# Modulation sums on TensorE, an earlier gather of expert rows, and another order of loads at the beginning

## The chip, the cores and the metric

The kernel runs on one core of a Trainium2 chip. The metric is the time of one execution on the device in microseconds (us). Five engines work side by side, each in the order of its own queue: PE (TensorE, matmuls into the eight banks of PSUM), DVE (VectorE), ACT (ScalarE), POOL (GpSimd) and SP (SyncE, which here only issues DMAs). Sixteen DMA engines move data between device memory and on-chip memory. A profile shows one execution; the share of full speed that the chip grants to PE is listed as PEclk (1.00 is 2.4 GHz, 0.50 is 1.2 GHz).

## What is computed

A trunk of two layers works on `x` (512 tokens of 1024 numbers, float32), steered by one vector `c` of 1024. Each layer derives six modulation vectors from `c`, mixes the tokens, and then sends each token through two of 32 experts:

```python
c_act = jax.nn.silu(c)
for layer in range(DEPTH):                       # two layers
    mod = c_act @ ada_w[layer] + ada_b[layer]    # 1024 x 6144 weights, 24 MB a layer
    shift1, scale1, gate1, shift2, scale2, gate2 = jnp.split(mod, 6, axis=-1)
    h = modulate(rmsnorm(x, norm1_w[layer]), shift1, scale1)
    # layer 0: h @ mix_w_in -> pooling channels, q, k, v; pooling and chunked attention; @ mix_w_out
    # layer 1: h @ ssm_w_in -> convolution, chunked state-space scan, gated norm; @ ssm_w_out
    x = x + gate1[:, None, :] * mix
    h2 = modulate(rmsnorm(x, norm2_w[layer]), shift2, scale2)
    # experts: top group of 4, top 2 of its 8 experts, silu(t @ w1) * (t @ w3), @ w2
    x = x + gate2[:, None, :] * ffn
return rmsnorm(x, final_norm_w)
```

## The kernel before

Tokens lie in four tiles of 128 rows. Most products of float32 numbers are split into a high and a low part of each operand (`split`, L108 to L113: ACT copies the high part, DVE or POOL subtracts to get the low one), and three matmuls add high by high, high by low and low by high. The framework orders the instructions of each engine by a model of costs, with the order of the program as priority; `manual_schedule` fixes the order by hand for the routing and for the end of each expert layer.

**Modulation.** A part of `ada_w` is 2048 columns wide. `ada` (L165) is a generator that loads eight pieces of 128 x 2048 (1 MB each) into a ring of five tiles (`w8`) and advances one piece at each call. A DVE instruction multiplies piece k by the column k of `c_act` and adds piece k-1; after the eighth, four matmuls with ones in 32 columns (L198) sum over the 128 partitions, and the bias row is added. In the even layer three such parts (`adas`: gate and router vectors of layer 0, and shift and scale of layer 1) are advanced at 25 places of the attention code (`fill`, with the counts in `FILL`). Two further parts run inside layer 1 and are not touched.

**The beginning (`even_mixer`).** SP issues the loads of `c`, of the four x tiles, of small vectors (`vrow`, `crow4`), and of the first 2048 modulation columns in two chunks of 512 + 512 columns (`ada_loads`), each followed by two loads of v weights. x is normalised and transposed by PE into `xa`; `ada_sums(b)` forms the sums of chunk b with the same DVE chain, `modulate(b)` applies them and splits the result into `h_hi` and `h_lo`; `v_products(b)` multiplies by the v weights: 8 pieces x 4 tiles x 3 matmuls. Then follow the dense products q0, k0, u0, u1, q1, ... (`Dense.next`, 24 matmuls each, L426 to L429), scores, transposes and values per pair of heads, and `out_proj` (`mo`). `late_loads` (L272 to L276) fetches three vectors of 32 numbers: `ssm_D` into `dcol`, number by number in a repeating pattern over 64 partitions twice, and `dtb` and `arow` repeated over 128 partitions. They are used in layer 1.

**Experts (`Moe.run`).** 17 units of two experts (16 pairs, and an overflow unit at position 8) run one after another. Unit u's hidden products come first, then `results(u - 1)`: y is written to the buffer `yd` in device memory, except for the units of the list `LAST` (units 8, 10, 13, 14, 15, 16), whose y is split and kept on chip with a one-hot matrix in `parts_y`. `products` multiplies the one-hot matrix by the kept y for each token tile, and `padd` (L1086) adds the result to x. For units 8, 10 and 13 this happens inside the loop two units later; units 14, 15 and 16 are the three operands of `combine` at the end. `ygather` (L1178) fetches the rows of `yd` by eight indirect DMAs on POOL that add into the four x tiles, two for each tile. It is issued in unit `GAT`. `combine` follows by hand: all products, then steps "x" (`padd`) and "h" (the next norm and transposes) in the order of `STEPS`. In layer 0, `ahead` loads and splits `wdt` (1024 rows of 32 numbers for layer 1) just before `combine`.

Of the kernel before, what the change touches and what calls it, by code (L numbers as in the profile page):

```python
# [36 lines left out]
GAT = 15  # L37
# [16 lines left out]
HOLD = 7  # L54
PINS = 3
# [7 lines left out]
LO = {"v": "G", "e": "VVG", "m": "V", "o": "GVV", "s": "VV"}  # L63
# [4 lines left out]
STEPS = "x0 h0 x1 h1 h0 x2 h2 h0 h1 x3 h2 h3 h3 h0 h1 h2 h1 w1 h3 w2 h3 h2"  # L68
# [7 lines left out]
def trunk_kernel(ctx, tc, x, c, ada_w, ada_b, norm1_w, norm2_w, mix_w_in, pool_w, pool_scale,  # L76
# [86 lines left out]

    def ada(layer, part, eng, first=None):
# [19 lines left out]
        load(1)  # L184
        for k in range(KD):
# [8 lines left out]
        for _ in range(SLACK):  # L194
            yield
        p = ps(name=f"pada{layer}{part}")
        for q in range(4):
            PE.matmul(p[32 * q:32 * q + 32, :], ones[:, 0:32], ws[KD - 1][:, q * 512:(q + 1) * 512], start=True,  # L198
                      stop=True, skip_group_check=True)
# [57 lines left out]
    pv = ps(name="pv")  # L257
    PE.transpose(pv[:, 0:P], vrow, ident)
    PE.transpose(pv[:, P:2 * P], crow4, ident)
    V.tensor_copy(vcol, pv[:, 0:P])  # L260
    V.tensor_scalar(cw.rearrange("p t k -> p (t k)"), pv[:, P:2 * P], 0.5, None, op0=ALU.mult)
# [4 lines left out]
    V.tensor_scalar(cb, vcol[:, 20:52], 0.5, None, op0=ALU.mult)  # L266
# [3 lines left out]

    def late_loads():
# [218 lines left out]
    def even_mixer(layer):  # L490
        with ExitStack() as es:
# [15 lines left out]
            def ada_loads(b):  # L507
                SP.dma_start(adb[0:64:32, b * 512:(b + 1) * 512], dap(ada_b, b * 512, [[D, 2], [1, 512]]))
                for k in range(0, KD, 2):
# [3 lines left out]
                    aw[b, k], aw[b, k + 1] = (t[:, d].rearrange("p q n -> p (q n)") for d in range(2))  # L513
# [26 lines left out]

            def modulate(b):
# [12 lines left out]
            def v_products(b):  # L554
                for kk in (4 * b, 4 * b + 2):
# [8 lines left out]
            def ada_sums(b):  # L564
                V.tensor_scalar(aw[b, 0], aw[b, 0], ccol[:, 0:1], None, op0=ALU.mult)
                for k in range(1, KD):
                    V.scalar_tensor_tensor(aw[b, k], aw[b, k], ccol[:, k:k + 1], aw[b, k - 1], op0=ALU.mult,
                                           op1=ALU.add)
                p = ps(name=f"pada00{b}")
                for q in range(2):  # L570
                    PE.matmul(p[32 * q:32 * q + 32, :], ones[:, 0:32], aw[b, KD - 1][:, q * 512:(q + 1) * 512],
                              start=True, stop=True, skip_group_check=True)
                m = adb[0:64, b * 512:(b + 1) * 512]
                V.tensor_add(m, p[0:64], m)
                p = ps((P, 4, 64), name=f"pm00{b}")
                for q in range(4):
                    PE.transpose(p[:, q, :], m[:, q * P:(q + 1) * P], ident[0:64, 0:64])
                ks = slice(4 * b, 4 * b + 4)
                V.scalar_tensor_tensor(ab[:, 0, 0, ks], p[:, :, 32], 1.0, n1w[0][:, ks], op0=ALU.add, op1=ALU.mult)
# [1225 lines left out]
```

## Time and profile before

| | |
|---|---|
| time, median of 3 runs | 1119.99 us (1119.96 to 1123.87) |
| profiled execution, its own time | 1120.03 us |
| its span, first to last instruction | 1118.3 us |
| mean granted PE clock | 0.932 |
| PE, DVE, ACT, POOL busy | 973.2, 800.3, 388.9, 300.2 us |
| DMA | 263.88 MB, mean 236 GB/s |

A line of the timeline gives start, duration, engine, line and operation, output <- inputs, shapes and, in brackets, how long the engine stood idle before and what released it. "x16" says that equal instructions in a row were merged. A float32 matmul that isn't split appears as two passes. A line with "q" after the engine's name (SPq) is an instruction that issues a DMA or waits.

### The profile page before, as it was taken

The page shows a single profiled execution, that of the slowest core. Times are in us where ns is not written, and L with a number is a line of the kernel's source. Part 1 is how long each engine was busy: PE and PEld are TensorE (multiplying, and loading weights), DVE is VectorE, ACT ScalarE, POOL GpSimd, SP SyncE. Part 2 cuts the span into 40 slices and gives each one's busy share as a digit, 9 for nine tenths or more (in the row PEclk, how much of TensorE's full clock was granted, in tenths as well). Part 3 has the DMA queues.
Part 4 walks back from the last instruction along what each step waited for, and adds up shares of the span by engine and source line. Part 5 has one row for each costly group of instructions (what it writes and reads, how often), then busy time and mean ns, then how long its engine had stood idle before and what let it go on. Part 6 is the DMA issues. An engine that isn't in the chain of part 4 may idle for free. (4 is left out here: it accounts for less than half of the span.)

```text
span 1118.3 us, 15578 instructions
## 1 busy us (share of the span) xinstructions
PE 973.2 (87%) x5474; PEld 729.5 (65%) x5474; DVE 800.3 (72%) x1650; ACT 388.9 (35%) x753; POOL 300.2 (27%) x329
## 2 busy tenths in 40 slices
PE   4588788699699996898999899899989999799994
PEld 3466466388556654776786777777766878556653
DVE  6717986654565874789997989887797555564976
ACT  3135332425123232433444333443433325222332
POOL 4413100204231122411513416244142004231124
PEclk9789888799799998899999999999999999799997
DMA  9476876598699979536473465554334945699987
GB/s 332 139 265 168 286 282 252 215 364 330 209 364 414 411 229 255 210 107 198 143 264 88 135 194 159 190 158 113 126 109 152 333 154 209 204 390 415 412 278 185
DMA packets 140200, 263.88 MB, mean 236 GB/s; under 512 B 19917, under 2 KB 82337, under 8 KB 134994
## 3 DMA queue, kind: packets, MB, share of 16 engines
q1 hardware_dynamic: 129122, 235.40, 60.1%
q0 software_dynamic: 8928, 20.97, 7.2%
q10 hardware_dynamic: 2064, 6.42, 1.4%
q8 instruction: 47, 0.77, 0.3%
q14 instruction: 39, 0.32, 0.1%
HBM read 254.19 MB, written 20.11 MB: 245 GB/s over the span
## 5 line engine op out<-in xcount | busy, mean ns | idle before, releaser
L1036 PE MATMUL ph<-w,xT 128*64 128x256 f32 (+1 forms) x1152 | 132.1, 374 | 0.9 <-DVE xT L1020 0.7
L1036 PEld LDWEIGHTS ph<-w,xT 128*64 128x64 f32 x1152 | 86.8, 139 | 51.8 <-issue 10.9
L189 DVE SCALAR_TENSOR_TENSOR ada<-ada,ccol,ada 128x2048 f32<-128x2048 f32 x35 | 87.1, 2489 | 0.2
L1003 POOL DMA_INDIRECT xg<-xnd,toks x32 | 32.3, 1008 | 149.8 <-PE pxt L1015 122.6
L1057 PE MATMUL pyy<-w,hidT 128*64 128x512 f32 x272 | 65.9, 605 | 4.2 <-ACT hidT L1049 4.2
L1038 ACT ACTIVATE th<-ph 128x128 f32<-128x128 f32 x34 | 9.4, 278 | 160.8 <-PE pht L1047 137.1
L1022 ACT ACTIVATE xT<-pxt,mc 128x128 f32<-128x128 f32 x136 | 51.3, 458 | 17.9 <-PE pxt L1015 10.9
L1062 DVE SCALAR_TENSOR_TENSOR y<-pyy,wsl,gate 128x512 f32<-128x512 f32 x68 | 48.1, 744 | 6.1 <-DMA yd<-y 4.5
L1015 PE MATMUL pxt<-ident,xg 128*128 128x128 f32 x272 | 37.9, 284 | 15.5 <-DVEq L1383 7.9
L1086 DVE TENSOR_TENSOR x<-x,pyc 128x512 f32<-128x512 f32 x64 | 40.4, 682 | 14.1 <-PE pyc L1079 8.0
L1039 DVE SCALAR_TENSOR_TENSOR th<-th,ph 128x128 f32<-128x128 f32 x34 | 9.8, 287 | 55.7 <-ACT th L1038 55.7
L1020 DVE TENSOR_SCALAR xT<-pxt,mc 128x128 f32<-128x128 f32 x136 | 46.6, 405 | 1.4 <-PE pxt L1015 1.4
L1581 DVE TENSOR_SCALAR ms<-lb,acs 128x128 f32<-128x128 f32 x128 | 41.0, 359 | 5.9 <-DMA lb<-acd 3.6
L1015 PEld LDWEIGHTS pxt<-ident,xg 128*128 128x128 f32 x272 | 34.5, 194 | 16.2 <-issue 15.6
L1548 DVE SCALAR_TENSOR_TENSOR cvx<-pdx,cw,cvx 128x511 f32<-128x511 f32 (+2 forms) x48 | 35.4, 738 | 6.7 <-ACT cvx L1545 6.6
L1178 POOL DMA_INDIRECT x<-yd,row x16 | 25.1, 1571 | 50.0 <-DMA xgfw<-in_final_norm_w_dram 22.3
L1584 POOL TENSOR_TENSOR ms<-ms,cbm 128x512 f32<-128x512 f32 x16 | 32.0, 2001 | 17.8 <-ACT ms L1583 16.0
L1057 PEld LDWEIGHTS pyy<-w,hidT 128*64 128x64 f32 x272 | 16.5, 136 | 28.1 <-issue 19.4
L1079 PE MATMUL pyc<-yh,yot 128*128 128x512 f32 x128 | 33.7, 398 | 1.0 <-DVE yot L1070 1.0
L469 DVE TENSOR_TENSOR sor<-sor,gate 128x1024 f32<-128x1024 f32 x16 | 20.4, 1276 | 18.0 <-DMA sor<-in_ssm_w_out_dram 17.9
L661 ACT ACTIVATE scs<-scs,mx 128x512 f32<-128x512 f32 (+3 forms) x32 | 17.7, 555 | 36.2 <-DVE mx L660 32.8
L1079 PEld LDWEIGHTS pyc<-yh,yot 128*128 128x128 f32 x128 | 23.4, 188 | 9.6 <-issue 1.9
(1074 smaller groups left out, 2778.4 us busy)
## 6 DMA issues: line engine op xcount, KB each, us to landing
w<-in_moe_w_dram SPq DMA_DIRECT2D x192, 512.0 KB
ada<-in_ada_w_dram SPq DMA_DIRECT2D x40, 1024.0 KB
yd<-y SPq DMA_DIRECT2D x22, 512.0 KB
ada<-in_ada_w_dram SPq DMA_DIRECT2D x16, 512.0 KB
wx<-in_ssm_w_in_dram SPq DMA_DIRECT2D x16, 512.0 KB
wz<-in_ssm_w_in_dram SPq DMA_DIRECT2D x16, 512.0 KB
lb<-acd SPq DMA_DIRECT2D x32, 256.0 KB
sor<-in_ssm_w_out_dram SPq DMA_DIRECT2D x16, 512.0 KB
```

What stands on the lines that cost most here:

```text
L189: a = eng.scalar_tensor_tensor(ws[k], ws[k], ccol[:, k:k + 1], ws[k - 1], op0=ALU.mult, op1=ALU.add)
L1003: d = GP.indirect_dma_start(out=xg, out_offset=None, in_=xnd[:, :], in_offset=bass.IndirectOffsetOnAxis(ap=idx, axis=0), bounds_check=T - ...
L1015: PE.transpose(p[:, q, :], xv[:, 4 * hf + q, :], ident)
L1020: V.tensor_scalar(xT[:, k, :], p[:, q, :], a, b, op0=ALU.mult, op1=ALU.add)
L1022: S.activation(xT[:, k, :], p[:, q, :], AF.Identity, bias=b, scale=a)
L1036: PE.matmul(ph[64 * j:64 * j + 64, n:n + h, :], xT[:, k, 64 * j:64 * j + 64], w13[n][:, :, k, :], start=k == 0, stop=k == KD - 1, skip_gro ...
L1057: PE.matmul(py[64 * j:64 * j + 64], hT[:, 64 * j:64 * j + 64], w2[:, s], start=True, stop=True, skip_group_check=True)
L1062: V.scalar_tensor_tensor(y[:, s], py, self.wsl[:, slot:slot + 1], self.gate2[:, s], op0=ALU.mult, op1=ALU.mult)
L1079: PE.matmul(p, part[2][:, i * P:(i + 1) * P], part[hf][:, q * 512:(q + 1) * 512], start=n + q == 0, stop=n == len(parts) - 1 and q == 1)
L1086: V.tensor_add(xst["x"][i][:, s], xst["x"][i][:, s], p)
L1548: V.scalar_tensor_tensor(a[:, sh:], p[:, :T - sh], cw[:, tap, ch:ch + 1], a[:, sh:], op0=ALU.mult, op1=ALU.add)
L1581: V.tensor_scalar(ms[:, h, :], lb[:, h, :], acs[:, cq, 4 * g + h:4 * g + h + 1], 0.0, op0=ALU.subtract, op1=ALU.min)
```

## The change

In the beginning and in the three parts of the even layer the modulation sums are formed by PE alone: the stationary operand is the column of `c_act` repeated 32 times, the moving operand the weights as loaded, and PSUM accumulates over the eight pieces. The two parts of layer 1 stay as they were. In the beginning the two pieces of a pair go to different groups of PSUM partitions, and the two halves are added after the transposes. The three short vectors are loaded as rows of 128 bytes into one partition and spread over the partitions by a product with ones. The transposes of the small vectors (`columns`) and the bias rows come later in the program; `ada_sums(1)` comes ahead of the v products; the low parts of the v weights and of all of h are subtracted by DVE. In the expert layers the gather is issued in unit 14, unit 13 becomes a fourth operand of `combine`, with the last operand separate for tiles 0 and 1, and two tiles come from the ring `w8`. In layer 0, `wdt` is loaded in unit 10 into another buffer and split by POOL at a new step `w0`.

```diff
-GAT = 15
+GAT = 14
+EARLY = 10
-LO = {"v": "G", "e": "VVG", "m": "V", "o": "GVV", "s": "VV"}
+LO = {"v": "V", "e": "VVG", "m": "V", "o": "GVV", "s": "VV"}
-STEPS = "x0 h0 x1 h1 h0 x2 h2 h0 h1 x3 h2 h3 h3 h0 h1 h2 h1 w1 h3 w2 h3 h2"
+STEPS = "x0 h0 x1 h1 h0 x2 h2 h0 h1 x3 h2 h3 h3 h0 h1 h2 h1 w0 w1 h3 w2 h3 h2"
...
+    def ada_mm(p, k, w, first, last):
+
+        for q in range(4):
+            PE.matmul(p[32 * q:32 * q + 32, :], ccol[:, k:k + 1].to_broadcast([P, 32]), w[:, q * 512:(q + 1) * 512],
+                      start=first, stop=last, skip_group_check=True)
...
             load(k + 2)
             yield
+            if not eng:
+                if not k:
+                    p = ps(name=f"pada{layer}{part}")
+                ada_mm(p, k, ws.pop(k), k == 0, k == KD - 1)
+                continue
...
+    def columns():
+
+        pv = ps(name="pv")
+        PE.transpose(pv[:, 0:P], vrow, ident)
+        PE.transpose(pv[:, P:2 * P], crow4, ident)
...
     def late_loads():
         SP.dma_start(yd[len(MAIN) * P:, :], zrow)
+        hrow = st_.tile([1, 3, 32], F32, name="hrow")
+        for n, src in enumerate((ssm_D, ssm_dt_bias, ssm_A_log)):
+            SP.dma_start(hrow[:, n, :], dap(src, 0, [[0, 1], [1, 32]]))
+        return hrow
+
+    def head_rows(hrow):
+
+        p = ps((P, 3, 32), name="phr")
+        PE.matmul(p, ones[0:1, :], hrow, start=True, stop=True)
         for q in range(2):
-            SP.dma_start(dcol[64 * q:64 * q + 64, :], dap(ssm_D, q, [[0, 64], [2, 16]]))
-        SP.dma_start(dtb, dap(ssm_dt_bias, 0, [[0, P], [1, 32]]))
-        SP.dma_start(arow, dap(ssm_A_log, 0, [[0, P], [1, 32]]))
+            V.tensor_copy(dcol[64 * q:64 * q + 64, :], p[64 * q:64 * q + 64, 0, q::2])
+        V.tensor_copy(dtb, p[:, 1, :])
+        V.tensor_copy(arow, p[:, 2, :])
...
-                    (V if g % 2 else GP).tensor_sub(parts[1][g], xa[g], parts[0][g].bitcast(F32))
+                    V.tensor_sub(parts[1][g], xa[g], parts[0][g].bitcast(F32))
...
             def ada_sums(b):
-                V.tensor_scalar(aw[b, 0], aw[b, 0], ccol[:, 0:1], None, op0=ALU.mult)
-                for k in range(1, KD):
-                    V.scalar_tensor_tensor(aw[b, k], aw[b, k], ccol[:, k:k + 1], aw[b, k - 1], op0=ALU.mult,
-                                           op1=ALU.add)
                 p = ps(name=f"pada00{b}")
...
+                for k in range(0, KD, 2):
+                    for d in range(2):
+                        for q in range(2):
+                            o = 64 * d + 32 * q
+                            PE.matmul(p[o:o + 32, :], ccol[:, k + d:k + d + 1].to_broadcast([P, 32]), aw[b, k][:, d, q],
+                                      start=k == 0, stop=k == KD - 2, skip_group_check=True)
...
             ada_loads(1)
             v_loads(1)
-            late_loads()
+            hrow = late_loads()
             ada_sums(0)
             modulate(0)
+            ada_sums(1)
             v_products(0)
-            ada_sums(1)
             modulate(1)
-            v_products(1)
+            v_products(2)
+            head_rows(hrow)
+            v_products(4, 6)
...
-            adas = [ada(0, 1, V), ada(0, 2, V), ada(1, 0, V)]
+            adas = [ada(0, 1, None), ada(0, 2, None), ada(1, 0, None)]
...
-                             self.parts_y[max(u - NPAIR + 2, 0)] if last(u) else None)
+                             self.parts_y[max(u - NPAIR + 3, 0)] if last(u) else None)
...
-                if 1 < u < NPAIR and last(u - 2):
+                if 1 < u < NPAIR - 1 and last(u - 2):
...
+                if u == EARLY and early:
+                    early()
...
-                p = [self.products(i, self.parts_y) for i in range(NT)]
+                p = self.products((0, 1), self.parts_y[:-1], False)
+                p = self.products((0, 1), self.parts_y[-1:], True, p)
+                p += self.products((2, 3), self.parts_y, True)
...
-                w = prev.y_tile("wdt")
-                wdt.append(w[:, 0:256].rearrange("p (k c) -> p k c", k=KD))
+
+            def early():
+                wdt.append(small.tile([P, KD, NLOG], F32, tag="wr", name="wdt", bufs=1)[:, :, 0:32])
                 SP.dma_start(wdt[0], w_in[:, 6144:6176].rearrange("(k p) c -> p k c", p=P))
+
+            def splits(n):
+                if n:
+                    return dense.split(n, GP)
                 wdt.append(ws4(F32R, "whl")[:, 0:512].rearrange("p (k c) -> p k c", k=KD))
-                split(wdt[1][:, :, 0:32], wdt[1][:, :, 32:64], wdt[0], V)
-
-            prev.run(ahead)
+                split(wdt[1][:, :, 0:32], wdt[1][:, :, 32:64], wdt[0], GP)
+
+            prev.run(ahead, early)
```

## Rows read from the trace of the kernel before

**Rows 1.** The page's part on the chain of waits that ended last: shares of the span by engine.

```profile
PE 7%; DMA 5%; DVE 1%; issue 0%; ACT 0%; POOL 0%; POOLq 0%; DVEq 0%; ACTq 0%; SPq 0%
```

**Rows 2.** Windows of the beginning: stretch, its length, busy time of PE, PE's weight loads, DVE, ACT and POOL (instructions), granted clock, busy share of the DMA engines, GB/s.

```profile
25.00:30.00 5.00, 2.58 (x8) 0.72 (x8) 2.94 (x3) 0.54 (x1) 5.00 (x2) 0.50 1.05 387
...
35.00:40.00 5.00, 2.84 (x7) 1.81 (x6) 4.96 (x3) 1.06 (x1) 4.97 (x2) 0.50 0.45 141
40.00:45.00 5.00, 5.00 (x19) 3.96 (x19) 4.89 (x4) 0.09 (x1) 1.06 (x1) 0.80 0.05 0
```

**Rows 3.** Timeline of SP's queue at 25 to 60 us.

```profile
30.99 3.52 SPq L274 DMA_DIRECT2D dcol<-in_ssm_D_dram  x2
34.56 3.66 SPq L275 DMA_DIRECT2D dtb<-in_ssm_dt_bias_dram  x1
...
41.09 4.32 SPq L402 DMA_DIRECT2D wq<-in_mix_w_in_dram  x1
```

**Rows 4.** The view of DMA queues at 40 to 45 us: all packets of the stretch, and how many are under each size.

```profile
DMA packets 540, 0.00 MB, mean 0 GB/s; under 512 B 540, under 2 KB 540, under 8 KB 540
```

**Rows 5.** Timelines of DVE, POOL, PE and ACT in the beginning: the last step of the first chunk's chain, the multiply and the result `ab` after it, the subtraction for h_lo on POOL, the first v product, the split of the first q weights.

```profile
23.88 1.28 DVE L567 SCALAR_TENSOR_TENSOR ada<-ada,ccol 128x1024 f32<-128x1024 f32 x1
...
27.83 2.90 DVE L565 TENSOR_SCALAR ada<-ada,ccol 128x1024 f32<-128x1024 f32 x1
...
30.72 0.14 DVE L580 COPY ab<-pm 128x4 f32<-128x4 f32 x1
...
34.45 3.31 POOL L550 TENSOR_TENSOR hlo<-xa,hhi 128x1024 fp32r<-128x1024 f32 x1 [4.27 <-ACT hhi L549]
...
34.42 0.79 PE L434 MATMUL accv<-vw0h,hhi 128*128 128x512 f32 x1 [5.60 <-ACT hhi L549]
...
58.99 1.06 ACT L110 ACTIVATE q0h<-wq 128x1024 fp32r<-128x1024 f32 x1 [13.02 <-DMA wq<-in_mix_w_in_dram]
```

**Rows 6.** The views of lines L532 (x products) and L434 (v products; duration in ns min/median/max, first and last start), and PE's timeline at the first k product and at the first output product.

```profile
L532 PE MATMUL pt<-dgx,x x64: 274/275/422, 11.6 to 20.1; 128*128 128x128 f32 x64
...
L434 PE MATMUL accv<-vw2h,hhi x8: 389/389/389, 44.9 to 49.6; 128*128 128x512 f32 x8
...
79.44 0.39 PE L426 MATMUL pdk<-hhi,k0h 128*128 128x512 f32 x1
...
221.21 0.96 PE L434 MATMUL mo<-mow0h,c 128*128 128x512 f32 x3
```

**Rows 7.** The four matmuls (eight passes) that end a modulation part: windows of line L198 alone (stretch, length, PE busy, weight loads, granted clock, DMA share, GB/s), and PE's timeline around one of them and around that of the beginning.

```profile
125.00:131.00 6.00, 1.93 (x8) 0.20 (x8) 0.50 1.02 389
784.00:786.00 2.00, 1.07 (x8) 0.16 (x8) 1.00 0.00 0
...
784.36 1.07 PE L198 MATMUL pada<-ada,ones 128*32 128x512 f32 x8
785.36 0.64 PE L235 MATMUL plb<-wr,mc 128*128 128x40 f32 x4
...
50.10 0.39 PE L436 MATMUL accv<-vw2h,hlo 128*128 128x512 f32 x1
50.42 1.05 PE L571 MATMUL pada<-ada,ones 128*32 128x512 f32 x4
```

**Rows 8.** One window from the first k product to the first output product; columns as in rows 2.

```profile
79.20:221.20 142.00, 114.22 (x526) 80.88 (x524) 108.72 (x223) 53.75 (x130) 24.52 (x21) 0.87 0.70 243
```

**Rows 9.** DVE's groups of instructions in the same stretch: busy us, mean ns | idle before.

```profile
L189 DVE SCALAR_TENSOR_TENSOR ada<-ada,ccol,ada 128x2048 f32<-128x2048 f32 x21 | 52.2, 2485 | 0.2
...
L191 DVE TENSOR_SCALAR ada<-ada,ccol 128x2048 f32<-128x2048 f32 x3 | 3.8, 1278 | 0.0
```

**Rows 10.** PE's longest waits in the same stretch: who waited for whom: us in total, times, longest.

```profile
PE pada L198 <- DVE ada L189: 9.1, 1, 9.1
PE sc L655 <- DVE c L111: 6.7, 1, 6.7
```

**Rows 11.** Timelines of PE, POOL, SP, ACT and DVE at the end of layer 0's experts: unit 13's products, the first gather, the load of `wdt`, the first final product, the split of `wdt` on ACT and DVE, the first adds to x.

```profile
407.02 3.94 PE L1079 MATMUL pyc<-yh,yot 128*128 128x512 f32 x16
...
409.34 1.60 POOL L1178 DMA_INDIRECT x<-yd,row  x1 [19.25 <-DVE x L1086]
...
417.17 0.38 SPq L1438 DMA_DIRECT2D wdt<-in_ssm_w_in_dram  x1
...
422.74 0.72 PE L1079 MATMUL pyc<-yh,yot 128*128 128x512 f32 x2
...
435.05 0.42 ACT L110 ACTIVATE whl<-wdt 128x256 fp32r<-128x256 f32 x1 [10.75 <-DMA wdt<-in_ssm_w_in_dram]
...
435.50 0.43 DVE L111 TENSOR_TENSOR whl<-wdt,whl 128x256 fp32r<-128x256 f32 x1 [9.45 <-ACT whl L110]
435.84 2.47 DVE L1086 TENSOR_TENSOR x<-x,pyc 128x512 f32<-128x512 f32 x4
```

**Rows 12.** The same at the end of layer 1's experts: the last write to `yd`, a window (columns as in rows 2), the first gather, the first add.

```profile
1070.17 0.33 SPq L1067 DMA_DIRECT2D yd<-y  x1
...
1080.00:1082.00 2.00, 2.00 (x16) 1.31 (x16) 2.00 (x5) 1.84 (x6) 0.53 (x1) 1.00 0.10 39
...
1081.47 1.60 POOL L1178 DMA_INDIRECT x<-yd,row  x1 [22.31 <-DMA xgfw<-in_final_norm_w_dram]
...
1098.70 1.28 DVE L1086 TENSOR_TENSOR x<-x,pyc 128x512 f32<-128x512 f32 x2 [4.06 <-DMA x<-yd,row]
```

More of the change, by code (lines that the diff above doesn't have):

```diff
@@ L193, in ada @@
                 tc.keep_in_program_order(a)
-        for _ in range(SLACK):
+        for _ in range(SLACK if eng else 0):
             yield
[L196 to L199, printed above, removed]
+        if eng:
+            p = ps(name=f"pada{layer}{part}")
+            for q in range(4):
+                PE.matmul(p[32 * q:32 * q + 32, :], ones[:, 0:32], ws[KD - 1][:, q * 512:(q + 1) * 512], start=True,
+                          stop=True, skip_group_check=True)
         m = b
@@ L512, in ada_loads @@
                         SP.dma_start(t[:, d], dap(ada_w, (k + d) * P * 6 * D + b * 512, [[6 * D, P], [D, 2], [1, 512]]))
-                    aw[b, k], aw[b, k + 1] = (t[:, d].rearrange("p q n -> p (q n)") for d in range(2))
+                    aw[b, k] = t
+                SP.dma_start(adb[0:64:32, b * 512:(b + 1) * 512], dap(ada_b, b * 512, [[D, 2], [1, 512]]))
             def v_loads(b):
@@ L539, in even_mixer @@
                             S.activation(dst, src, AF.Copy)
+            columns()
             def modulate(b):
@@ L580, in ada_sums @@
-                V.tensor_copy(ab[:, 0, 1, ks], p[:, :, 0])
+                two = st_.tile([P, 2, 4], F32, name=f"two{b}")
+                V.tensor_copy(two, p[:, :, 0:64:32].rearrange("p q n -> p n q"))
+                V.tensor_add(two, two, p[:, :, 64:P:32].rearrange("p q n -> p n q"))
+                V.scalar_tensor_tensor(ab[:, 0, 0, ks], two[:, 1], 1.0, n1w[0][:, ks], op0=ALU.add, op1=ALU.mult)
+                V.tensor_copy(ab[:, 0, 1, ks], two[:, 0])
             ada_loads(1)
             v_loads(1)
-            late_loads()
+            hrow = late_loads()
@@ L1071, in results, with products @@
                                     op0=ALU.add, op1=ALU.is_equal)
-        def products(self, i, parts):
-            ps2 = [ps(name=f"pyc{self.layer}{i}{hf}") for hf in range(2)]
-            for hf, p in enumerate(ps2):
-                for n, part in enumerate(parts):
-                    for q in range(2):
-                        PE.matmul(p, part[2][:, i * P:(i + 1) * P], part[hf][:, q * 512:(q + 1) * 512],
-                                  start=n + q == 0, stop=n == len(parts) - 1 and q == 1)
-            return ps2
+        def products(self, tiles, parts, stop=True, sums=None):
+            out = sums or [[ps(name=f"pyc{self.layer}{i}{hf}") for hf in range(2)] for i in tiles]
+            for i, ps2 in zip(tiles, out):
+                for hf, p in enumerate(ps2):
+                    for n, part in enumerate(parts):
+                        for q in range(2):
+                            PE.matmul(p, part[2][:, i * P:(i + 1) * P], part[hf][:, q * 512:(q + 1) * 512],
+                                      start=not sums and n + q == 0, stop=stop and n == len(parts) - 1 and q == 1,
+                                      skip_group_check=True)
+            return out
         def padd(self, i, ps2):
@@ L1451, in after @@
                     yield from hT_tile(layer, i, h_hi, h_lo)
-                prev.combine([after(i) for i in range(NT)], STEPS, lambda n: dense.split(n, GP))
+                prev.combine([after(i) for i in range(NT)], STEPS, splits)
                 prev.close()
```

38 lines of the change are left out of this document (16 added, 22 removed).

## The prediction

> **What bounds the kernel now.** The chain of waits that ended last comes first, and it explains little: its shares add up to about 13% of the span [rows 1], all of it in the second MoE layer. So I read the stages that the diff touches one by one, in windows of time, and asked in each which wait ends last.
>
> *Beginning.* The DMA engines move about 387 GB/s up to 35 us; then the rate falls to 0 at 40 to 45 us with a busy share of 0.05 [rows 2]. In those 5 us 540 packets moved no measurable volume [rows 4]: single numbers of 4 bytes, the column loads of `dcol` (2 x 64 x 16 = 2048 of them), followed by `dtb` and `arow`. 2048 at 108 per us are 19 us. SP's queue shows the same: `dcol` and `dtb` hold it for 3 to 4 us each, and `wq`, issued at 41.09 behind them [rows 3], is split only at 58.99, after ACT waited 13.02 us for it [rows 5]. PE meanwhile has two holes: it starts the v products at 34.42, because DVE's multiply-add chain for the first modulation chunk ends at 25.2 and its result `ab` comes at 30.87 behind a DVE multiply that took 2.90 us [rows 5]; and it waits for `wq`. The granted clock is 0.50 of full (1.2 GHz) at 25 to 40 us, after PE had been nearly idle [rows 2].
>
> *Even layer, from the first k product (79.44) to the first output product (221.21) [rows 6].* 142 us: PE 114.2 busy at mean clock 0.87, DVE 108.7 busy [rows 8], of which 52.2 + 3.8 = 56.0 are the three modulations' multiply-adds [rows 9]. PE's longest waits are for DVE: 9.1 us for the last modulation, 6.7 for an attention result that stands behind others in DVE's queue [rows 10]. DVE bounds this stage.
>
> *Ends of the MoE layers.* In layer 0 DVE's first add to x comes at 435.84, right behind the split of `wdt`, for which ACT waited 10.75 us; PE began the products at 422.74 [rows 11]. In layer 1 the first add, at 1098.70, waits for the gather [rows 12].
>
> **The change part by part.**
>
> *A, to the first k product.* Each modulation chunk in the beginning becomes 4 visits of PE (two k in each, four column groups of 32). A visit is 8 passes: 1.07 us at clock 1.00, 1.93 at 0.50 [rows 7]; start to the next instruction's start is 785.36 - 784.36 = 1.00 us. So a chunk costs 4 us. The x products end at 20.4 [rows 6]; the chunk's data are in before 23.9, since DVE begins its last step then without a wait [rows 5]. PE is done by about 23.5; add, four transposes and the small DVE steps, about 3 us by those of before, give `ab` at 26.5. From `ab` to the first v product took 34.42 - 30.87 = 3.55 us, so that product starts at 30. Then PE owes 96 v products at 0.224 us ((49.6 - 44.9) / 21 steps [rows 6]) = 21.5, the second chunk's 4, its transposes 1, some 2 for clock not yet back, and 24 q products, 5.4: 63.9 in place of 79.44, so **-15**. The wait for `hlo`, 3.31 us on POOL [rows 5], shrinks to a DVE subtraction, and `wq` has 20 us to land. Ends: -19 (full clock throughout) and -5 (the second chunk's sum stands ahead of the v products on PE and lands late, and q still waits). The new row loads are three of 128 bytes; the product that spreads them and its four small copies, about 1.5 us in all, lie beside the v products. Moving `columns()` and the bias rows costs nothing: DVE, which loses 16 steps of 1.28 us, covers it; uncovered, 1 us.
>
> *B, even layer.* DVE loses 56.0 us. PE gains 24 visits and loses 3: 21 x 1.00. At full clock PE's work of before is 114.2 x 0.87 = 99.4; new 120.4. Before, 142 - 99.4 = 42.6 us went to idling and slow clock, mostly behind DVE. I leave a third, 14, for attention's own latency: 134.4, so **-8**. Ends: -20 (almost nothing left over) and +10 (31 of the 42.6 stay). Here a wait is added: a modulation product waits for its 1 MB of weights, and behind it on PE stand the q, k and u products and the scores, for which ACT and DVE wait. The tile ring is 5 deep and the DMA share is 0.70 [rows 8], so I count that inside the 14. The accumulators now hold one PSUM bank through eight steps; that is inside the +10.
>
> The row for entering a visit: the matmul before one starts at 50.10, the visit at 50.42 [rows 7], 0.32 against a pitch of 0.224, so 0.10 us are lost. The Trainium skill, TensorEngine Tiling (Array Packing), section Tiling Modes, speaks against the change: switching the tiling mode drains the array. By that rule 24 visits pay on the way in as well as out; the trace agrees with 0.10 in, which would make B 24 x 0.10 = 2.4 us dearer; the way out is already in the 1.00.
>
> *C, end of layer 0.* `wdt` is loaded in unit 10 and split later, on POOL. So the first add no longer waits for it. Unit 13's 16 products (3.94 us at 407.02) leave the loop, so unit 16 ends 3.9 earlier and PE can start the final products at 418.8. For tiles 0 and 1 it does 24 of them (5.4) and then 8 with the last operand (1.8): tile 0 is ready at 425.3, tile 1 at 426.1, the others 3.6 us apart. Gathers: they stood behind unit 13's adds (POOL waited for DVE until 409.34); now they start one unit earlier, as soon as `yd` has landed. The first add therefore comes at about 425.4 for 435.84: **-10**. Ends: -4 (gathers still last) and -12. The moved `wdt` load has 1024 rows of 128 bytes in a stage full of weights: nothing by the ring of weights ahead of PE, 9.5 us at the rate of [rows 4]; I take 0. Its split costs 0.43 us on DVE [rows 11], at most 3.31 / 4 = 0.8 on POOL, ahead of the next split: 0.5 of the 10.4 is given back.
>
> *D, end of layer 1.* The last `yd` write is issued at 1070.17 and DMA is still draining at 1080 (share 0.10 at 1080 to 1082); the first gather starts at 1081.47 [rows 12]. One unit earlier in the program is thus worth 0 to 3 us: **-1**, or +2 if gathers and last loads collide. PE's final products, 14.5 us from about 1088, end before the last add either way.
>
> **The sum.** -15 - 8 - 10 - 1 = -34. The profiled execution took 1120.03 us (span 1118.3), the median is 1119.99, so no correction between them: **1086**. Its own range, with the parts' ends taken half, is 1075 to 1097.
>
> **Rivals.**
> 1. *The freed time is only partly passed on:* A brings 5 because the second chunk still sets the v products, B nothing because PE, now the fuller engine, keeps its holes; C stands, D 1 and 2 us elsewhere: 1120 - 18 = 1102. For it: PE is in order, and loads set the pace to 37 us. Against: most holes name DVE or `wq`. 20%.
> 2. *PE packs almost perfectly:* A -19, B -18, C -10, D -2: 1071. For it: nearly all long waits end on DVE. 12%.
> 3. *The cuts don't reach the end:* B's new PE work (+10) and late gathers (C -4) eat A (-5 to -7): about 1119. For it: three bounds trade places. Against: `wdt` and `dcol` are plain. 5%.
> 4. *Slower: PE stands still for weights.* A 1 MB chunk takes 2.7 us at 387 GB/s [rows 2]. If PE waits that long at each of the 24, B becomes 99.4 + 24 x 2.7 + 14.8 (slow clock as before) = 179, +37: 1120 - 26 + 37 = 1131. It decides from B = +26, that is 168 us or about 2 us of waiting per chunk beyond the 120.4. For it: the fill steps bunch five and then nine chunks. Against: DVE before waited 0.2 us for these weights [rows 9]. 7%.
>
> **How the numbers follow.** Forecast 56%, rivals 20, 12, 5 and 7%. The range from 1070 to 1107 holds the forecast, rival 1 and half of rival 2. A change under 0.5% (5.6 us) cannot be told from none. Faster 0.88 (forecast, rivals 1 and 2), same 0.05, slower 0.07.
>
> **What would show it.** A: no window without DMA volume between 37 and 55 us, and the first k product near 64. B: DVE busy about 53 us in that stage, PE about 120 at a clock above 0.95, no long PE wait on a weight load. C: the first x add of layer 0 about 10 us less after the loop's end, ACT not waiting for `wdt`. D: the first gather soon after the last `yd` write. The prediction is wrong if PE's waits in the even layer name DMA, or if the stage is longer than 152 us.

## The result and the profile after

The changed kernel takes 1092.45 us (median of four runs, 1089.55 to 1097.40) where the kernel before took 1120.91 on the same chip: a ratio of 0.9746, 95% interval 0.9705 to 0.9787. Two later sessions gave 0.9776 (0.9711 to 0.9841), where 0.972 to 0.977 had been expected, and 0.9748 (0.9722 to 0.9775). The forecast was 1086, the range 1070 to 1107. The profiled execution took 1092.9 us (span 1091.2), 27.1 us less span than before.

The table follows starts of single instructions through both traces. Differences accumulate down the page, so a step's own gain is the change from the row above.

| milestone | before | after | difference | forecast |
|---|---|---|---|---|
| first v product | 34.42 | 38.18 | +3.8 | -4 |
| first k product | 79.44 | 66.13 | -13.3 | -15 (A) |
| first scores | 85.73 | 74.35 | -11.4 | |
| first output product | 221.21 | 202.40 | -18.8 | -23 (A, B) |
| layer 0: first expert product | 291.83 | 273.48 | -18.4 | |
| layer 0: first of unit 8's products | 367.22 | 350.19 | -17.0 | |
| layer 0: first add to x | 435.84 | 410.88 | -25.0 | -33 (A to C) |
| `dt`'s transposed products (pdtt) | 470.84 | 444.33 | -26.5 | |
| layer 1: last write of `yd` | 1070.17 | 1042.26 | -27.9 | |
| layer 1: first gather | 1081.47 | 1053.18 | -28.3 | |
| layer 1: first add to x | 1098.70 | 1071.64 | -27.1 | -34 (A to D) |

Windows of the beginning, after (columns as in [rows 2]):

```profile
25.00:30.00 5.00, 3.60 (x16) 0.88 (x16) 3.56 (x9) 2.98 (x4) 0.00 (x0) 1.00 1.04 384
...
35.00:40.00 5.00, 3.86 (x20) 2.07 (x17) 2.12 (x7) 1.92 (x3) 0.53 (x1) 1.00 0.47 173
40.00:45.00 5.00, 5.00 (x24) 4.14 (x23) 3.84 (x5) 3.63 (x4) 0.00 (x0) 1.00 0.48 139
```

The window at 40 to 45 us, which moved nothing before, now moves 139 GB/s. A shorter gap is left: at 38 to 42 us, in windows of 1 us, 0 to 8 GB/s are moved, and `wq` is issued at 41.30, after SP waited 4.0 us for DVE to free a v weight buffer. The granted clock at 25 to 40 us is 1.00 (2.4 GHz) where it was 0.50 (1.2 GHz): PE's sums keep it busy ahead of the v products, and in the run below with these sums on DVE it is 0.50 again. PE's timeline of the same stretch:

```profile
20.97 3.64 PE L598 MATMUL pada<-ada,ccol 128*32 128x512 f32 x32
25.62 0.63 PE L604 MATMUL pm<-ident,adab 128*128 128x128 f32 x4 [1.02 <-DVE adab L601]
...
27.77 1.05 PE L598 MATMUL pada<-ada,ccol 128*32 128x512 f32 x4 [0.36 <-DMA ada<-in_ada_w_dram]
...
35.91 1.05 PE L598 MATMUL pada<-ada,ccol 128*32 128x512 f32 x4 [0.30 <-DMA ada<-in_ada_w_dram]
37.80 0.63 PE L604 MATMUL pm<-ident,adab 128*128 128x128 f32 x4 [0.84 <-issue]
38.18 0.48 PE L460 MATMUL accv<-vw0h,hhi 128*128 128x512 f32 x1
```

The first chunk is summed in one go. The second goes at the pace of its loads, 1.36 us a piece, and stands ahead of every v product, which so begin at 38.18.

The even layer in one window, and PE's waits in it (answers to [rows 8, 10]):

```profile
66.13:202.40 136.27, 126.63 (x694) 79.72 (x692) 55.35 (x200) 53.95 (x129) 21.91 (x20) 0.97 0.74 259
```

```profile
PE pm L309 <- DVE adab L215: 3.1, 1, 3.1
PE sc L687 <- ACT kT L728: 2.6, 1, 2.6
...
PE pada L168 <- DMA ada<-in_ada_w_dram: 0.9, 1, 0.9
```

DVE went from 108.7 us to 55.4, PE is busy 93% of the stage, and it waited 0.9 us in all for the weights of its new sums, the only wait of the stage that names DMA: rival 4 did not come. Both layers' ends, on SP, POOL and DVE (answers to [rows 11, 12]):

```profile
381.61 0.33 SPq L1099 DMA_DIRECT2D yd<-y  x1
...
392.53 1.59 POOL L1215 DMA_INDIRECT x<-yd,row  x1 [19.48 <-DVE xT L1052]
...
410.88 1.28 DVE L1120 TENSOR_TENSOR x<-x,pyc 128x512 f32<-128x512 f32 x2 [6.62 <-DMA x<-yd,row]
...
1042.26 0.33 SPq L1099 DMA_DIRECT2D yd<-y  x1
...
1053.18 1.67 POOL L1215 DMA_INDIRECT x<-yd,row  x1 [22.28 <-issue]
...
1071.64 1.29 DVE L1120 TENSOR_TENSOR x<-x,pyc 128x512 f32<-128x512 f32 x2 [9.55 <-DMA x<-yd,row]
```

In both layers the first gather starts 10.9 us after the last write of `yd`; before it was 11.3 in both (409.34 and 1081.47 in [rows 11, 12], the writes at 398.04 and 1070.17). "One unit earlier" moved the gathers by 0.4 us here (in layer 0 by 1.0 and 1.4 us in two other profiles of this kernel), and the first add now waits for them in layer 0 too, where `wdt` was last before.

The trace also records when each write's last piece landed. In the kernel before that was 406.76 in layer 0 and 1080.43 in layer 1, now it is 391.53 and 1052.18. So the gather follows the landing by 1.0 us, except in layer 0 of the kernel before, where it came 2.6 us later, behind the adds of unit 13 on DVE that [rows 11] names.

### The profile page after: what moved, and what is told of

Same layout as the page of the kernel before. It is cut to its first block, busy times and chain, and to the rows that moved or that the text cites. A ratio compares the mean times of both kernels' runs of the same rounds, so it can differ in the third digit from the quotient of the medians.

```text
span 1091.2 us, 15960 instructions
## 1 busy us (share of the span) xinstructions
PE 985.3 (90%) x5700; PEld 725.7 (67%) x5700; DVE 718.6 (66%) x1607; ACT 388.4 (36%) x753; POOL 285.2 (26%) x324
## 2 busy tenths in 40 slices
DMA packets 137840, 263.88 MB, mean 242 GB/s; under 512 B 17555, under 2 KB 79975, under 8 KB 132632
## 5 line engine op out<-in xcount | busy, mean ns | idle before, releaser
L1054 ACT ACTIVATE xT<-pxt,mc 128x128 f32<-128x128 f32 x136 | 51.1, 456 | 17.2 <-PE pxt L1047 11.7
L1120 DVE TENSOR_TENSOR x<-x,pyc 128x512 f32<-128x512 f32 x48 | 30.4, 683 | 23.5 <-DMA x<-yd,row 19.3
L202 DVE SCALAR_TENSOR_TENSOR ada<-ada,ccol,ada 128x2048 f32<-128x2048 f32 x14 | 35.0, 2497 | 0.1
L495 DVE TENSOR_TENSOR sor<-sor,gate 128x1024 f32<-128x1024 f32 x16 | 20.4, 1276 | 17.3 <-DMA sor<-in_ssm_w_out_dram 17.3
L1627 ACT ACTIVATE ms<-ms 128x512 f32<-128x512 f32 x32 | 19.9, 624 | 24.1 <-DVE ms L1625 24.0
L1675 PE MATMUL pyd<-ms,xdt 128*64 128x128 f32 x256 | 19.7, 287 | 9.3 <-DVE ms L1628 9.3
L1642 PE MATMUL pxd<-ident,cvx 128*128 128x128 f32 x64 | 11.8, 320 | 17.7 <-DVE cvx L1596 17.7
```

What stands on the lines that cost most here:

```text
L1054: S.activation(xT[:, k, :], p[:, q, :], AF.Identity, bias=b, scale=a)
```

## The experiments

Each kernel is the changed one with the edit shown, unless its text says otherwise. Ratios are to the kernel before in the same session. Since totals of one kernel differ by some us (see the last section), stages are compared by starts in the traces, beside three profiles of the changed kernel (called the three below).

**DVE's chains back in the even layer.**

```diff
-            adas = [ada(0, 1, None), ada(0, 2, None), ada(1, 0, None)]
+            adas = [ada(0, 1, V), ada(0, 2, V), ada(1, 0, V)]
```

> The changed kernel with the three modulations of the even layer on DVE again (multiply-add chains), everything else as changed. Theory (DVE bounds that stage, and the change moved the bound to PE): the stage from the first k product to the first output product grows from 136.3 us back to 141 to 144 us, DVE's busy time in it from 55 to about 108 us, and the run from about 1092 to 1097 to 1100 us. Rival (with the beginning mended, the stage is set by something else, the full clock having brought what was gained): the stage stays within 2 us of 136.3 and the run within 3 us of the changed kernel's.

Ratio 0.9809 (0.9764 to 0.9855), 1097.5 us. The stage's window and PE's longest waits:

```profile
65.51:206.63 141.12, 114.41 (x526) 80.97 (x524) 108.30 (x222) 54.33 (x130) 23.46 (x20) 0.88 0.71 247
```

```profile
PE pada L212 <- DVE ada L202: 7.7, 1, 7.7
PE sc L687 <- DVE c L112: 6.5, 1, 6.5
PE pdq L452 <- DVE mx L690: 5.8, 1, 5.8
```

All three waits name DVE again and the clock falls back to 0.88. The stage is 141.1 us beside 135.2 to 136.5 in the three: B is worth 4.6 to 6.0 us, and DVE's load was its cause. The totals alone would not settle it, since the intervals overlap.

**The short vectors loaded as before.**

```diff
-        hrow = st_.tile([1, 3, 32], F32, name="hrow")
-        for n, src in enumerate((ssm_D, ssm_dt_bias, ssm_A_log)):
-            SP.dma_start(hrow[:, n, :], dap(src, 0, [[0, 1], [1, 32]]))
-        return hrow
+        for q in range(2):
+            SP.dma_start(dcol[64 * q:64 * q + 64, :], dap(ssm_D, q, [[0, 64], [2, 16]]))
+        SP.dma_start(dtb, dap(ssm_dt_bias, 0, [[0, P], [1, 32]]))
+        SP.dma_start(arow, dap(ssm_A_log, 0, [[0, P], [1, 32]]))
...
-            head_rows(hrow)
```

> The changed kernel with the three small vectors loaded number by number again (2048 + 4096 + 4096 numbers, as before), without the product that spreads them. Theory (the hole in the DMA volume lies behind the v weights and ahead of wq, and PE has v products until 60.7 us, so the hole is mostly covered now): the first k product moves from 66.1 to 67 to 70 us, the run by +1 to +4 us. Rival (the hole is on the path, as the 13 us wait for wq in the kernel before suggests): the first k product at 74 us or later, the run +8 us or more.

Of the numbers in this expectation only the 2048 of `dcol` are loaded singly: the page lists 19917 packets under 512 bytes where the changed kernel's has 17555, 2362 more and not 10240, and `dtb` and `arow` go as rows of 128 bytes.

Ratio 0.9868 (0.9830 to 0.9906), 1104.7 us: the dearest single undo. The first k product stays at 66.21; the loss comes behind it, as a window (columns as in [rows 2]) and PE's and ACT's timelines show:

```profile
45.00:50.00 5.00, 5.00 (x23) 4.13 (x22) 0.96 (x1) 0.00 (x0) 0.00 (x0) 1.00 0.05 0
```

```profile
82.77 3.84 PE L686 MATMUL sc<-kT,qT 64*128 64x512 f32 x16 [10.96 <-ACT kT L727]
...
58.72 1.06 ACT L111 ACTIVATE q0h<-wq 128x1024 fp32r<-128x1024 f32 x1 [14.02 <-DMA wq<-in_mix_w_in_dram]
...
76.83 1.06 ACT L111 ACTIVATE u1h<-wu 128x1024 fp32r<-128x1024 f32 x1 [6.58 <-DMA wu<-in_mix_w_in_dram]
81.17 1.06 ACT L111 ACTIVATE q1h<-wq 128x1024 fp32r<-128x1024 f32 x1 [3.29 <-DMA wq<-in_mix_w_in_dram]
82.14 0.58 ACT L727 ACTIVATE kT<-pdk 128x512 f32<-128x512 f32 x1
```

`kT`, which the scores need, stands on ACT behind two splits, and these wait for late loads. With 0 GB/s from 40 to 50 us the splits of the later weights come 7.5 to 9.6 us later than in the changed kernel; the products ahead of them cover that up to the first k product and no further. The first scores come 8.2 to 8.4 us later than in the three, the first output product 8.2 to 9.4. The rival had the size, and neither had the place.

**Only the row loads, in the kernel before.**

```diff
+        hrow = st_.tile([1, 3, 32], F32, name="hrow")
+        for n, src in enumerate((ssm_D, ssm_dt_bias, ssm_A_log)):
+            SP.dma_start(hrow[:, n, :], dap(src, 0, [[0, 1], [1, 32]]))
...
-            SP.dma_start(dcol[64 * q:64 * q + 64, :], dap(ssm_D, q, [[0, 64], [2, 16]]))
-        SP.dma_start(dtb, dap(ssm_dt_bias, 0, [[0, P], [1, 32]]))
-        SP.dma_start(arow, dap(ssm_A_log, 0, [[0, P], [1, 32]]))
...
-            late_loads()
+            hrow = late_loads()
...
+            head_rows(hrow)
             v_products(1)
```

> The kernel before with nothing but the three row loads in place of the loads number by number, and the product and copies that spread them. Theory (the hole in the DMA volume was the larger part of what the beginning gained: the second and third column loads cost the changed kernel 8.4 us at the first scores): the first scores at 76 to 79 us for 85.7 in the kernel before, and the run -6 to -9 us, about 1112. Rival (PE's late start behind DVE's sums, at half clock, is what sets the first scores): the first scores move by less than 3 us and the run by less than 3.

Ratio 0.9933 (0.9915 to 0.9952), 1115.3 us: -7.5 us by the ratio. First scores 79.51, a little past the expected 76 to 79, first output product 214.8 for 221.2. SP's and ACT's timelines, and one of SP's waits in the kernel before, correct the reading of [rows 3]:

```profile
31.01 0.24 SPq L275 DMA_DIRECT2D hrow<-in_ssm_D_dram  x1
...
41.10 0.39 SPq L411 DMA_DIRECT2D wq<-in_mix_w_in_dram  x1
...
50.23 1.06 ACT L110 ACTIVATE q0h<-wq 128x1024 fp32r<-128x1024 f32 x1 [4.37 <-PE accv L444]
```

```profile
SPq L402 <- POOL vw4l L111: 2.2, 1, 2.2
```

`wq` is issued at 41.10, as before at 41.09: SP waits there for a weight buffer, which POOL frees, not for the column loads. What these cost was the landing. By the trace's records `wq` landed at 44.98 here and at 58.89 before; it is split at 50.23, when ACT waits for PE, and at 58.99 in [rows 5], when ACT waited for the load.

**The first layer's sums on DVE again.** `ada_sums` and the views of its weights as before, and the order:

```diff
+            v_products(0, 2)
             ada_sums(1)
-            v_products(0)
             modulate(1)
-            v_products(2)
             head_rows(hrow)
```

> The changed kernel with the first layer's modulation sums on DVE again in the beginning, in the old order (sum and modulation of the second chunk behind the first 48 v products), the row loads kept. Theory (with the hole gone these sums are the smaller part): the first scores at 76 to 79 us for 74.4 in the changed kernel, the run +2 to +4 us. Rival (PE's sums are most of the gain in the beginning): the first scores at 81 us or later, the run +7 us or more.

The first scores come at 83.98, 9.4 to 9.6 us later than in the three; the first output product at 210.3 for 201.6 to 202.8. By the stage the rival is right, but this is not PE's sums alone: the low parts of the v weights stay on DVE, where the change had put them. A window (columns as in [rows 2]), SP's longest wait and DVE's timeline in this kernel, and POOL's timeline in the kernel before:

```profile
40.00:45.00 5.00, 5.00 (x24) 4.14 (x23) 4.89 (x5) 1.06 (x1) 0.00 (x0) 0.99 0.00 0
```

```profile
SPq L428 <- DVE vw4l L112: 10.0, 1, 10.0
```

```profile
31.70 0.73 DVE L593 TENSOR_SCALAR ada<-ada,ccol 128x1024 f32<-128x1024 f32 x1
...
44.59 1.22 DVE L112 TENSOR_TENSOR vw4l<-vr,vw4h 128x1024 fp32r<-128x1024 f32 x1
```

```profile
37.78 3.28 POOL L111 TENSOR_TENSOR vw4l<-vr,vw4h 128x1024 fp32r<-128x1024 f32 x1
```

On DVE the low part `vw4l` comes behind the second chunk's sums, at 44.59; on POOL it came at 37.78. SP's queue stands 10.0 us until DVE has done it and a weight buffer is free, so the DMA window is empty again, although no number is loaded singly: an empty window alone does not tell which of the two causes it has. In the kernel with only the row loads, which has the sums on DVE and the low parts on POOL, the first scores came at 79.51. So about 5 of the 9.5 us are left for the sums themselves; the other 4.5 go with the low parts on DVE and the smaller moves of the beginning, none of which was undone by itself.

The low parts have a price on POOL too: DVE's multiply at the head of the second chunk's sum took 2.90 us in [rows 5], while POOL subtracted `vw2l` (27.34 to 30.18 in its timeline), and 0.73 here, with POOL idle. No run isolates this.

The total shows less of the loss: 1099.2 us beside 1095.5 of the changed kernel in the same session (0.9785, 0.9746 to 0.9824). In these two profiles the odd layer (last section) took 368.0 us here and 374.1 in the changed kernel.

**The second chunk's sum behind the first v products.**

```diff
+            v_products(0)
             ada_sums(1)
-            v_products(0)
             modulate(1)
```

> The changed kernel with the second chunk's modulation sum behind the first 24 v products on PE instead of ahead of all of them. Theory (that order is why the v products began at 38.2 instead of the predicted 30, and it costs the path): the first v product at 29 to 31 us, the first k product at 59 to 62 us for 66.1, and the run -4 to -6 us. Rival (ACT's splits wait for the weights of u and q, so the loads set the first scores): the v and k products come as much earlier, but the first scores stay within 1.5 us of 74.4 us and the run within 2 us.

The v products begin at 29.16, as the prediction had it, the first k product at 63.82, the first scores at 70.11; but the first output product stands at 202.63. Ratio 0.9762 (0.9692 to 0.9833) beside 0.9776: no difference. PE met this wait:

```profile
75.66 0.79 PE L452 MATMUL pdu<-hhi,u0h 128*128 128x512 f32 x1 [3.12 <-DVE mx L690]
```

By the first pooling product, 92.70 us beside 92.62, 93.77 and 94.22 in the three, at most 1.5 us of the gain were left, and none at the first output product (201.6 to 202.8 in the three). Theory and rival each had half: the scores moved 4 us and the run did not. What sets that later point was not isolated.

**Unit 13 in the loop and the gathers in unit 15.** The operand tiles and the final products are as before too.

```diff
-GAT = 14
+GAT = 15
...
-                             self.parts_y[max(u - NPAIR + 3, 0)] if last(u) else None)
+                             self.parts_y[max(u - NPAIR + 2, 0)] if last(u) else None)
...
-                if 1 < u < NPAIR - 1 and last(u - 2):
+                if 1 < u < NPAIR and last(u - 2):
```

> The changed kernel with unit 13 in the loop and the gathers in unit 15 again, as before. Theory (the first gather follows the last write of yd by 11 us in both kernels, because the write must land; where it stands in the program does not matter, and the first x add waits for gathers): the first gather still comes about 11 us after the last write of yd in both layers, and the run changes by 0 to +2 us. Rival (the prediction: the gathers stood behind unit 13's adds on DVE, and unit 13's products lay on the path): the first x add of layer 0 comes 4 us or more later against the loop, and the run is +4 to +9 us.

Ratio 0.9752 (0.9706 to 0.9799): nothing lost. The first gather follows the last write by 11.30 us in layer 0 and 10.91 in layer 1. From unit 8's products to pdtt: 94.6 us, beside 93.7 to 94.1 in the three and 103.6 before. The theory's reason holds for layer 1 only. In layer 0 the gather waits for unit 13's adds again, as POOL's timeline shows:

```profile
393.57 1.59 POOL L1214 DMA_INDIRECT x<-yd,row  x1 [19.25 <-DVE x L1120]
```

The write had landed at 391.48, and the gather comes 2.1 us later, 1.1 more than behind a landing alone. The rival had the wait right and its size wrong.

**`wdt` loaded and split as before.**

```diff
+                w = prev.y_tile("wdt")
+                wdt.append(w[:, 0:256].rearrange("p (k c) -> p k c", k=KD))
                 SP.dma_start(wdt[0], w_in[:, 6144:6176].rearrange("(k p) c -> p k c", p=P))
...
-                split(wdt[1][:, :, 0:32], wdt[1][:, :, 32:64], wdt[0], GP)
+                split(wdt[1][:, :, 0:32], wdt[1][:, :, 32:64], wdt[0], V)
...
-            prev.run(ahead, early)
+            prev.run(ahead)
```

> The changed kernel with wdt loaded at the end of the loop and split ahead of the first x add on ACT and DVE again, as before. Theory (that wait was nearly all of the gain at the end of layer 0): the first x add of layer 0 comes 7 to 10 us later than in the changed kernel's 410.9 us, behind ACT's wait for wdt, and the run is +6 to +10 us. Rival (the gathers are last there anyway, and give the end of the layer): the first x add moves by less than 3 us and the run by 0 to +3 us.

Ratio 0.9762 (0.9733 to 0.9790), unit 8 to pdtt 95.4 us: the theory fell. SP's and POOL's timelines and SP's wait show why:

```profile
379.50 0.33 SPq L1099 DMA_DIRECT2D yd<-y  x1
388.37 0.38 SPq L1477 DMA_DIRECT2D wdt<-in_ssm_w_in_dram  x1
...
389.36 1.60 POOL L1215 DMA_INDIRECT x<-yd,row  x1 [17.81 <-issue]
```

```profile
SPq L1477 <- DMA yd<-y: 8.5, 1, 8.5
```

Here `wdt`'s buffer comes free at 388.37, ahead of the gathers, and the load is in before anyone needs it. The same rows give the landing of the last `yd` write, 8.9 us after its issue, and the first gather 1.0 us behind it.

**Both undone.** The edits of the last two together.

> The changed kernel with both parts of the end of layer 0 undone: unit 13 in the loop and the gathers in unit 15, and wdt loaded at the end of the loop and split on DVE ahead of the first x add. Theory (each part alone takes away the same wait: with unit 13 out of the loop wdt's buffer comes free before the gathers, and with the early load it does not matter when it comes free): ACT waits for wdt again, the first x add of layer 0 comes 8 to 10 us later than in the changed kernel, and the run is +8 to +10 us, though each part undone alone cost 2 us or less. Rival (the parts add up): the run is +1 to +3 us, and the gain at the end of layer 0 came from elsewhere.

Unit 8 to pdtt takes 103.1 us, which is the 103.6 of before, against 93.7 in the changed kernel of the same session: +9.4, though the parts cost 0.4 to 0.9 and 1.3 to 1.7 alone. SP's longest wait, and the timelines of SP, ACT and DVE:

```profile
SPq L1474 <- DVE yh L112: 18.7, 1, 18.7
```

```profile
398.08 0.38 SPq L1474 DMA_DIRECT2D wdt<-in_ssm_w_in_dram  x1
...
415.46 0.42 ACT L111 ACTIVATE whl<-wdt 128x256 fp32r<-128x256 f32 x1 [10.26 <-DMA wdt<-in_ssm_w_in_dram]
...
416.25 2.47 DVE L1120 TENSOR_TENSOR x<-x,pyc 128x512 f32<-128x512 f32 x4
```

With unit 13 in the loop the buffer waits for DVE's split of a result (as in [rows 11], where the load went out at 417.17), and the load goes out 7.8 us after the first gather (390.24). Either edit alone takes `wdt` out of that place. The run lost only 3.9 us (1101.5 beside 1097.6; 0.9807 and 0.9776, with intervals that overlap); the odd layer was 6.0 us shorter in this kernel's profile than in the other.

**The last two `yd` writes from ACT's queue.**

```diff
-                             self.parts_y[max(u - NPAIR + 3, 0)] if last(u) else None)
+                             self.parts_y[max(u - NPAIR + 3, 0)] if last(u) else None, S if u > 10 else SP)
```

> The changed kernel with the last two writes of yd in each MoE layer (units 11 and 12) issued from ACT's queue instead of SP's. Theory (the end of both layers is set by the landing of the last yd write, which stands behind the last expert weights in SP's queue): the first gather comes 3 to 6 us earlier against the loop in both layers, the last adds of layer 1 as much, and the run is -4 to -9 us. Rival (the landing is set by the load on the DMA engines, or the gathers wait for something else): the first gather still comes 10 to 11 us after that write, and the run stays within 2 us.

Ratio 0.9706 (0.9642 to 0.9770), 1090.9 us beside 1097.6. The first gather follows the last write by 3.9 us in layer 0 and 7.3 in layer 1. In layer 1, from unit 8's products to the first add: 58.1 us for 63.4. In layer 0 nothing is won at pdtt (93.7). The kernel once more, beside the changed kernel:

> The kernel with the last two writes of yd from ACT's queue once more, for a closer interval beside the changed kernel in the same call. Theory (5.4 us at the end of layer 1, nothing at the end of layer 0, where PE's last products are then in front): 4 to 7 us under the changed kernel. Rival (part of the 6.7 us seen was the odd layer's clock, which differs between executions of one kernel): 2 us or less.

> The changed kernel unaltered, as the measure of this call: a ratio to the kernel before of 0.973 to 0.978.

1089.65 us (ratio 0.9700, 0.9673 to 0.9726) beside 1095.51 (0.9748): 5.9 us faster than the changed kernel, the intervals all but apart. ACT, POOL and DVE at the end of layer 1:

```profile
1045.20 0.33 ACTq L1099 DMA_DIRECT2D yd<-y  x1
...
1051.20 1.60 POOL L1215 DMA_INDIRECT x<-yd,row  x1 [14.16 <-DMA w<-in_moe_w_dram]
...
1072.21 2.48 DVE L1120 TENSOR_TENSOR x<-x,pyc 128x512 f32<-128x512 f32 x4 [3.99 <-PE pyc L1112]
```

The first gather now comes 6.0 us after the write, for 11.0 in the changed kernel's profile taken beside it, and the first add waits for PE's products instead. The write itself is issued 33.5 us after unit 8's products for 34.4, so for the gather 0.9 us come from the issue and 5.0 from the landing (3.0 and 3.6 in the first of the two runs). Of that the first add keeps 4.0, and from unit 8's products to the end of the run it is 79.5 us for 84.0; the rest of the 5.9 lies elsewhere, the odd layer's 371.2 us for 374.1 among it. This is the fastest kernel of the study. The Trainium skill, DMA: Bandwidth & Descriptors, has two sections on this: Queues, rings and completion order says that each DMA engine takes turns between the queues that have work, Issuing engines are not separate DMA queues that a second issuing engine saves only the time of issuing. The runs bear out the first and not the second: the landing brought the gather 5.0 of 6.0 us, and 3.6 of 6.6 in the first of the two runs, the issue the rest.

## Why the prediction was right, and where it was off

The forecast's sum was -34; the span fell by 27.1. By its steps:

*A, -15, measured -13.3 at the first k product and -11.4 at the first scores.* The terms were not right one by one. "That product starts at 30" failed: it started at 38.18, by the low end's reason ("the second chunk's sum stands ahead of the v products on PE and lands late"). It cost little, because the 4 us of that sum and the 1 of its transposes, which the forecast had behind the start, now lay ahead of it; because the 2 us for the clock did not come, as it was 1.00 throughout; and because `wq` was in time. So PE ran from 38.18 to 66.13 without the two holes, 27.95 us for the forecast's 33.9. That the two errors nearly cancel at the first k product is in part luck. One sum is off by itself: four visits behind 20.4 end at 24.4, not "by about 23.5"; they ended at 24.61. Putting the second sum later did not shorten the run. "`wq`, issued at 41.09 behind them" read an order as a cause: SP waited for a buffer, and the column loads' price was the late landing of all that followed. The 1.9 us lost between the k product and the scores are PE's wait for `kT`, 2.6 us for 0.7 before, the place where `col_loads` lost its time too. Undone, the loads cost 8.2 to 9.4 us at the first output product, and the sums 7.5 to 8.7 together with the low parts that the change had put on DVE.

*B, -8, measured -5.5 (136.27 for 141.8).* The 14 us left to latency came out at 136.27 less 126.63 x 0.97 = 122.8, so 13.4: that is luck, since "a third" stood on no row. PE's work was mis-sized, 122.8 for 120.4. The terms that failed are two: the way in, which the prediction priced at 2.4 and left out of the sum, and "the way out is already in the 1.00":

```profile
160.65 0.39 PE L455 MATMUL pdk<-hhi,k3l 128*128 128x512 f32 x1
160.97 1.06 PE L168 MATMUL pada<-ada,ccol 128*32 128x512 f32 x8
161.97 0.50 PE L452 MATMUL pdk<-hhi,k3h 128*128 128x512 f32 x1
162.30 0.39 PE L454 MATMUL pdk<-hlo,k3h 128*128 128x512 f32 x1
```

At a pitch of 0.224 the way in costs 0.10 (0.32) and the matmul behind the visit another 0.11 (0.33). Visits in a row take 0.86 each and 0.13 once: five of them, from 83.76 to the next product at 88.19, take 4.43. PE entered 17 times in the stage: 24 x 0.86 + 17 x (0.13 + 0.21) = 26.4, less the three visits of before at 1.21, is +22.8 for the forecast's 21. The Trainium skill, TensorEngine Tiling (Array Packing), section Tiling Modes, says that a switch of tiling mode drains the array. The trace fits this with 0.10 us on the way in and 0.11 on the way out; no run separates the switch from the change of operands.

*Between B and C, 1.8 us were lost* (-18.8 to -17.0), most of it in the first expert units, where PE waited 8.4 us for gathered tokens and 2.2 for DVE's transposed ones (7.6 and 0.7 before); another 1.4 were gained between pdtt and the last write. The forecast had no term for either. In two other profiles of the changed kernel 0.7 and 0.9 us were lost, and the stretch from pdtt to the last write was 5.4 and 5.5 us longer than before (last section), so neither is firm.

*C, -10, measured -8.0 at the first add and -9.5 at pdtt.* The size was right, the account of it half. PE came as forecast: where the gathers are early enough (the kernels with the writes on ACT's queue), the first add stands 58.0 us behind unit 8's products, for 68.6 before, 10.6 earlier and waiting for PE. The step that failed is "now they start one unit earlier, as soon as `yd` has landed". The reading behind it was right, POOL did wait for unit 13's adds; but the write had landed only 2.6 us ahead of the gather, which comes 1.0 behind any landing, so at most 1.6 were to be had. In this profile none came, since the write took 9.9 us to land for 8.7: the first gather stands 42.3 us behind unit 8's products, for 42.1 before (41.1 and 40.7 in two other profiles). So "tile 0 is ready at 425.3" no longer set the first add: it waits for tile 0's second gather, the low end's case, at 60.7 us behind unit 8's products (58.9 in the two others). The gain is `wdt`'s wait, and either of two edits takes it away.

*D, -1, measured +0.8* between the last write (-27.9) and the first add (-27.1): the gathers started 0.4 us sooner behind the write and took 18.5 us to the first add for 17.2.

Rival 1 (1102) was the nearest of the rivals in size, but not in kind: B did pass something on. Rivals 2 to 4 did not happen. The sum's own range is added up wrongly: "with the parts' ends taken half" the ends of A to D give 1076 to 1104, not 1075 to 1097; the measured 1092 lies in both.

## What to carry to other kernels

Before pricing an instruction that is moved earlier, ask what it waits for: a gather that needs a write to land gained 0 to 1.4 us from an earlier place in the program, while the write, on a queue without the last weights in front of it, brought the run 6. Undo the parts of a change together as well as alone: two parts that mend the same wait each look worthless when undone singly. And an idle stretch of a DMA queue has two readings, a buffer that is not free and transfers that do not finish; the issue time against the landing time tells them apart.

## What I had not expected of the hardware

The odd layer's time differs between executions of one kernel, and its granted clock with it. From pdtt to the first output product of that layer the changed kernel took 368.4, 373.9 and 374.1 us in the three, at a mean clock of 0.97, 0.95 and 0.95. Windows of the first two (columns as in [rows 2]):

```profile
490.00:500.00 10.00, 6.55 (x43) 4.87 (x42) 10.00 (x14) 2.76 (x4) 0.00 (x0) 1.00 0.72 240
500.00:510.00 10.00, 10.00 (x51) 8.44 (x50) 9.56 (x21) 4.78 (x7) 3.07 (x2) 1.00 0.60 174
```

```profile
490.00:500.00 10.00, 6.40 (x39) 4.67 (x38) 10.00 (x15) 2.76 (x4) 0.00 (x0) 0.85 0.78 256
500.00:510.00 10.00, 10.00 (x38) 8.06 (x37) 6.98 (x15) 2.88 (x4) 2.41 (x1) 0.81 0.36 111
```

PE is busy 6.4 to 6.6 us of the first window in both, and the clock falls in one: the rows show the lower clock and not its reason. It hides or adds up to 6 us, as much as most edits here are worth: the stage says what an edit did, the total alone does not. Of the 14 profiles of this study, the four that reach the stage before 444.0 us took 371.2 to 374.1 us for it; of the ten that reach it later, eight took 366.9 to 368.9 and two 371.3 and 374.1. Whether a kernel that comes earlier to this layer meets the lower clock more often, and so gives back a part of what it gained, stays open.

A visit of four 32-column sums costs PE 1.2 us alone and 0.86 in a row. The 17 entries of the even layer cost 17 x 0.34 = 5.8 us; bunching the sums was not tried.
